# Gate of y in four stages, pooling products kept apart from x and added in the SSD half

## The chip, the cores and the metric

One core of one Trainium2 chip runs the whole program; the time is the device time of that core in microseconds (us). The core has a matmul engine (PE, TensorE), three engines for elementwise work (DVE, ACT, POOL) and a queue, SP, which issues nearly every transfer (DMA) of this kernel, in order. PE writes its results into eight PSUM banks; everything else lies in SBUF tiles. A profile is one execution of the program with its instructions recorded.

## The reference

One layer of a hybrid decoder in float32, for 1056 tokens (1024 of a prompt, 8 x 4 of a decode group). Width 1024, FFN width 2816. What matters here is the mixer and what stands behind it:

```python
x = x + 0.5 * swiglu(rms_norm(x, norm_ffn1), ...)        # FFN1
proj = rms_norm(x, norm_mix) @ w_in                        # z | xBC | dt | pool
y, h = ssd_scan(xs, dtp, a, bm, cm, h0)                     # the scan
y = rms_norm((y + d_skip * xs) * silu(z), ssd_norm_w)       # gate by z, then a norm
yp = multiscale_pool(pool_ext, n_valid, pool_w, pool_scale)
x = x + concat([y, yp], axis=-1) @ w_out                    # w_out has 2048 rows
x = x + 0.5 * swiglu(rms_norm(x, norm_ffn2), ...)           # FFN2
x = x + sigmoid(rms_norm(x, norm_ple) @ ple_gate) * (p @ ple_proj)
y = rms_norm(x, final_norm)
```

The product with `w_out` is taken in two halves: the pooling half (rows of yp) and the SSD half (rows of y). The norm of y is a factor for each token, so the SSD half is multiplied by it after its matmuls.

## The kernel before

Tensors lie with the 1024 channels as eight blocks of 128 partitions (index `m` for output blocks) and tokens along the free side. Tokens are cut into `CH`, pieces of 384, 384 and 288, or into four pieces of `CQ` = 264. float32 accuracy comes from splitting each operand into a high and a low part; `three` (L258) takes three matmul passes for each of eight channel blocks, so one product of one output block with one piece of tokens is 24 matmuls. A weight block is loaded by SP as 512 KB (L216) and split by an ACT cast (L235) and a DVE subtraction (L236).

The stages around the change, in order of time:

- **Scan.** `scan()` runs 16 units. Between them `products()` yields one product at a time (loop at L1259): 24 of z (evicted from their bank by an ACT copy, L1218, and stored to `d_z`) and 24 of the pooling half. A product of the pooling half loads its piece of x from `d_x` (L1232), adds it to the bank on DVE (L1235) and stores the sum to `d_x` (L1236). The scan has 35 yields, so 11 products of the pooling half lie in it and 13 are left. While `products()` runs it has three banks, `nacc[0] = 3`.
- **Mixed stage.** The while loop after the scan takes one product of the pooling half and two steps of `gated()` a turn. `gated()` has 24 steps (three pieces of tokens x eight blocks): it loads z (L1244) and y (L1245), multiplies z by the norm of x on POOL (L1246), takes Silu on ACT (L1247), multiplies y by it on DVE (L1248), splits the result into `yh` (ACT, L274) and `yl` (DVE, L275), squares it on ACT (L1251) and adds the square to `acc` on DVE (L1253). A step takes three buffers of a ring of 13 (`tmp`).
- **SSD half.** L1290 to L1308: eight blocks of four pieces of 264 tokens, 32 products of 24 matmuls on `yh` and `yl`, now with all eight banks, from bank 0 on. Each one loads x (L1298), multiplies the bank by the norm `R1` on DVE (L1301), adds x on POOL (L1302), stores x (L1303), and splits the sum for FFN2 (ACT L274, DVE L275); an ACT square (L282) and a POOL addition (L283) gather the squares for the next norm. The three matmuls of the norm (L289, bank 7) stand among the first four products, each one ahead of the first use of its piece.
- **FFN2's first blocks.** Matmuls L507 write banks 0 to 3 first, then 4 and 5. x is loaded once more (L540) once the ring of buffers is released, and the second norm (L289 to L294) follows.

The order of PE is written out by hand everywhere. The orders of POOL, DVE and ACT are written by hand in the scan and in parts of the FFNs; in the mixed stage and the SSD half a tile scheduler sets them, and that of SP everywhere.

Of the kernel before, what the change touches and what calls it, by code (L numbers as in the profile page):

```python
# [15 lines left out]
P = 128  # L16
D = 1024
KB = 8
# [65 lines left out]
def emit(tc, dr):  # L84
# [25 lines left out]
    def f(o, n, p0=0, p1=P):  # L110
        return o.f[p0:p1, o.c : o.c + n]
# [33 lines left out]
    d_z = dp.tile([P, KB, T], F32, name="d_z")  # L145
    d_yp = dp.tile([P, KB, T], F32, name="d_yp")
    d_yf = dp.tile([P, KB, T], F32, name="d_yf")
    d_ac = dp.tile([P, P], F32, name="d_ac")
    d_acs = dp.tile([H, TS], F32, name="d_acs")

# [5 lines left out]
    def tmp(n):  # L156
        cnt["T"] += 1
        return tslots[cnt["T"] % len(tslots)]
# [1034 lines left out]
    def products():  # L1193
# [32 lines left out]
        for m in range(8):  # L1226
            w = next_w()
            for c0, n in CH:
                while groups and groups[0][1][0] <= c0:
                    take()  # L1230
                t = tslots[4] if m == 0 else tmp(n)
                SY.dma_start(f(t, n), d_x[:, m, c0 : c0 + n])  # L1232
                ps = bank()[:, 0:n]
                gemm_X(ps, w, c0, n)
                V.tensor_tensor(f(t, n), ps, f(t, n), op=ALU.add)  # L1235
                SY.dma_start(d_x[:, m, c0 : c0 + n], f(t, n))  # L1236
                yield

    def gated():

        for c0, n in CH:
            for m in range(8):
                z, yz, q = tmp(n), tmp(n), tmp(n)
                SY.dma_start(f(z, n), d_z[:, m, c0 : c0 + n])  # L1244
                SY.dma_start(f(yz, n), d_yf[:, m, c0 : c0 + n])  # L1245
                G.tensor_tensor(f(z, n), f(z, n), f(o_R0 + c0, n), op=ALU.mult)  # L1246
                S.activation(f(z, n), f(z, n), AF.Silu)  # L1247
                V.tensor_tensor(f(yz, n), f(yz, n), f(z, n), op=ALU.mult)  # L1248
                split_gain(L["yh"] + (m * T + c0), L["yl"] + (m * T + c0), f(yz, n), vec(V_SSD + m), n)
                acc = f(L["acc"] + c0, n)  # L1250
                S.activation(f(q, n) if m else acc, f(yz, n), AF.Square)  # L1251
                if m:
                    V.tensor_tensor(acc, acc, f(q, n), op=ALU.add)  # L1253
                yield

    a, b = scan(), products()
# [17 lines left out]
    while a is not None or b is not None:  # L1274
        if b is not None and next(b, done) is done:
            b = None
        for _ in range(2):
            if a is not None and next(a, done) is done:
                a = None
    later_norm(L["R1"])  # L1280

    def R1_at(c0, n):
        for a, na in CH:
            if a in pending and a < c0 + n:
                finish_norm(*pending.pop(a))
        return f(L["R1"] + c0, n)


    nacc[0] = 8
    cnt["acc"] = 0  # L1290
    for m in range(8):
        w = next_w()
        if m == 7:
            load_raw("wgu2", 0)
        for k in range(4):
            h, c, c0, n = k // 2, k % 2, CQ * k, CQ
            xr, t = tmp(n), tmp(n)
            SY.dma_start(f(xr, n), d_x[:, m, c0 : c0 + n])  # L1298
            ps = bank()[:, 0:n]
            three(ps, [((w(i, 0), w(i, 1)), (r(o_yh + (i * T + c0), n), r(o_yl + (i * T + c0), n))) for i in range(KB)])  # L1300
            V.tensor_tensor(f(t, n), ps, R1_at(c0, n), op=ALU.mult)  # L1301
            G.tensor_tensor(f(t, n), f(t, n), f(xr, n), op=ALU.add)  # L1302
            SY.dma_start(d_x[:, m, c0 : c0 + n], f(t, n))  # L1303
            o = piece(half(m % 2, h), m // 2) + CQ * c
            split_gain(o, o + TH, f(t, n), vec(V_FFN2 + m), n)
            square_into(f(t, n), c0, n, m == 0)
            if m == 7 and k < 2:
                weights1("wgu2", 0, L7["W2"], k)  # L1308
    load_raw("wgu2", 1)


# [185 lines left out]
```

## Time and profile before

| | |
|---|---|
| time, median of 3 runs | 2324.18 us (2323.12 to 2325.68) |
| profiled execution | 2321.62 us, of which the span of the trace is 2319.9 |
| PE busy | 2242.5 us, 97% of the span |
| DVE, ACT, POOL busy | 1436.6, 792.7, 482.8 us (62%, 34%, 21%) |
| chain that ended last | PE 83%, DVE 8%, issue 4%, DMA 3%, ACT 2%, POOL 1% |
| mixed stage | 1294.35 to 1357.33 us |
| SSD half | 1357.33 to 1455.41 us, then FFN2 |

PE is the engine that sets the time, with gaps in a few places. The profiled execution lies 2.56 us below the median of the runs shown; 1.7 us of it lie around the span. A busy PE is not always at full speed: the granted clock (PEclk, 1.00 is full) is read beside it. Times of instructions on POOL are rough. Where the text says what an engine waited for, it is the releaser that the trace infers from semaphores.

### The profile page before, as it was taken

What the parts mean: (1) busy time and instruction counts of PE and PEld (TensorE: products, weight loads), DVE (VectorE), ACT (ScalarE), POOL (GpSimd) and SP (SyncE); (2) the same over time, 40 slices, a digit from 0 to 9 for tenths busy, and PEclk for the clock granted to TensorE, in tenths of its full rate; (3) what the DMA queues carried; (4) which work ended last, traced back from release to release, by engine and by line L of the source; (5) the groups of instructions that cost most, each with busy time, mean ns of one, the idle gap of its engine ahead of it and who ended that gap; (6) DMA issues with size and microseconds to landing.
All of it is one profiled execution on the core that took longest, in us unless ns stands there. A gap on an engine that the chain in (4) does not pass through costs nothing.

```text
span 2319.9 us, 38096 instructions
## 1 busy us (share of the span) xinstructions
PE 2242.5 (97%) x15651; PEld 2188.1 (94%) x15651; DVE 1436.6 (62%) x2113; ACT 792.7 (34%) x1331; POOL 482.8 (21%) x416
## 2 busy tenths in 40 slices
PE   8999999999999999999979989999999999999997
PEld 8999999999999999977858889999999999999996
DVE  7776666663345856545777764576766666334566
ACT  6422222231123124223453543342222233112455
POOL 1122222200003420022222335112222220001343
PEclk9999999999999999999989999999999999999999
DMA  5422122282122233344354654432221227221243
GB/s 185 140 79 79 67 82 84 78 268 84 60 83 85 70 90 68 49 136 144 117 155 135 201 171 140 178 123 79 83 79 69 80 91 255 83 76 44 72 148 130
DMA packets 155711, 257.48 MB, mean 111 GB/s; under 512 B 56784, under 2 KB 101008, under 8 KB 150032
## 3 DMA queue, kind: packets, MB, share of 16 engines
q1 hardware_dynamic: 155536, 255.04, 34.5%
q8 instruction: 123, 2.02, 0.3%
q14 instruction: 52, 0.43, 0.1%
HBM read 195.42 MB, written 59.57 MB: 110 GB/s over the span
## 4 chain that ended last, share of the span: by engine, by line
PE 83%; DVE 8%; issue 4%; DMA 3%; ACT 2%; POOL 1%; SPq 0%; DVEq 0%; ACTq 0%; POOLq 0%
PE bank L258 42%; PE pair L390 32%; PE bank L507 5%; PE bank L1162 1%; DVE Wa L1004 1%; DMA Wa<-d_ac 1%; DVE wl L1150 1%; ACT xs L1014 1%; PE bank L1064 1%; DVE Wa L1105 1%; DMA tmp<-d_z 1%; DMA raw<-wgu 0%; DVE W L379 0%; PE bank L875 0%; PE bank L289 0%
## 5 line engine op out<-in xcount | busy, mean ns | idle before, releaser
L258 PE MATMUL bank<-X,W 128*128 128x384 f32 (+1 forms) x4320 | 730.3, 325 | 17.2 <-DVE W L236 5.3
L258 PEld LDWEIGHTS bank<-X,W 128*128 128x128 f32 x4320 | 702.5, 189 | 21.6 <-DVE W L236 6.0
L390 PE MATMUL pair<-X,W 128*128 128x264 f32 x3648 | 458.4, 285 | 0.2 <-DVE n L415 0.2
L390 PEld LDWEIGHTS pair<-X,W 128*128 128x128 f32 x3648 | 450.8, 188 | 0.5 <-DVE n L415 0.4
L390 PE MATMUL pair<-E,W 128*128 128x264 f32 x1824 | 234.9, 285 | 0.0
L390 PEld LDWEIGHTS pair<-E,W 128*128 128x128 f32 x1824 | 227.5, 188 | 0.0
L488 DVE SCALAR_TENSOR_TENSOR x<-bank,x 128x384 f32<-128x384 f32 (+1 forms) x192 | 99.4, 523 | 205.9 <-PE bank L258 203.7
L258 PE MATMUL bank<-E,W 128*128 128x384 f32 (+1 forms) x1200 | 217.3, 323 | 0.0
L258 PEld LDWEIGHTS bank<-E,W 128*128 128x128 f32 x1200 | 197.0, 188 | 0.0
L283 POOL TENSOR_TENSOR acc<-acc,tmp 128x384 f32<-128x384 f32 (+2 forms) x89 | 82.6, 928 | 498.2 <-ACT tmp L282 498.2
L379 DVE TENSOR_TENSOR W<-ws,W 128x512 fp32r<-128x512 f32 x152 | 129.8, 855 | 46.0 <-ACT W L378 45.8
L507 PE MATMUL bank<-X,W 128*128 128x264 f32 x1152 | 146.4, 289 | 6.8 <-DVE acc L292 2.1
L507 PEld LDWEIGHTS bank<-X,W 128*128 128x128 f32 x1152 | 144.2, 192 | 9.2 <-DVE acc L292 2.7
L459 ACT CAST W<-raw 128x640 fp32r<-128x640 f32 (+1 forms) x64 | 50.0, 782 | 249.4 <-PE bank L258 211.2
L420 POOL TENSOR_TENSOR cg<-cg 128x528 f32<-128x528 f32 x38 | 76.0, 2001 | 255.4 <-issue 227.2
L378 ACT CAST W<-ws 128x512 fp32r<-128x512 f32 x152 | 93.1, 615 | 92.0 <-PE pair L390 84.2
L390 PE MATMUL pair<-nd,W 128*128 128x264 f32 x912 | 119.5, 288 | 3.6 <-DVE p L409 3.6
L390 PEld LDWEIGHTS pair<-nd,W 128*128 128x128 f32 x912 | 115.7, 191 | 4.0 <-DVE p L409 4.0
L378 ACT CAST W<-raw 128x512 fp32r<-128x512 f32 x114 | 70.9, 622 | 141.4 <-DMA raw<-wgu 107.1
L258 PE MATMUL bank<-nd,W 128*128 128x384 f32 (+1 forms) x576 | 108.3, 323 | 0.0
L258 PE MATMUL bank<-yh,W 128*128 128x264 f32 x512 | 96.8, 291 | 5.9 <-DVE tmp L1235 5.9
L235 ACT CAST W<-raw 128x1024 fp32r<-128x1024 f32 (+2 forms) x65 | 60.5, 930 | 123.2 <-PE bank L258 109.6
(305 smaller groups left out, 3000.8 us busy)
## 6 DMA issues: line engine op xcount, KB each, us to landing
raw<-wgu SPq DMA_DIRECT2D x43, 1024.0 KB, 4.8
hraw<-d_h SPq DMA_DIRECT2D x44, 528.0 KB, 3.9
d_h<-cg SPq DMA_DIRECT2D x76, 264.0 KB, 2.0
raw<-win SPq DMA_DIRECT2D x28, 512.0 KB, 5.3
raw<-wd SPq DMA_DIRECT2D x32, 384.0 KB, 3.1
raw<-wd SPq DMA_DIRECT2D x32, 320.0 KB, 3.0
Wa<-d_ac SPq DMA_DIRECT2D x16, 512.0 KB, 3.9
raw<-wout SPq DMA_DIRECT2D x16, 512.0 KB, 3.8
```

The lines of the kernel that those rows point to most:

```text
L235: S.copy(r(o_w, n), f(o_r, n))
L258: PE.matmul(ps, lhsT=a, rhs=b, start=i == 0, stop=i == n - 1)
L283: eng.tensor_tensor(f(L["acc"] + c0, n), f(L["acc"] + c0, n), f(o_q, n), op=ALU.add)
L378: S.copy(r(o, 512), f(src, 512))
L379: V.tensor_tensor(r(o + 512, 512), f(src, 512), f(o, 512), op=ALU.subtract)
L390: PE.matmul(ps, lhsT=r(w + (512 * p + P * q), P), rhs=r(x + TH * b, CQ), start=first and q == 0 and j == 0, stop=q == 3 and j == 2, skip_g ...
L420: G.tensor_tensor(f(o_u1, TH), f(o_u1, TH), f(o_g, TH), op=ALU.mult)
L459: S.copy(r(o, n), src)
L488: V.scalar_tensor_tensor(xm, ps, 0.5, xm, op0=ALU.mult, op1=ALU.add)
L507: PE.matmul(ps, lhsT=r(w, P), rhs=r(piece(half(j, h), q) + (TH * b + CQ * c), CQ), start=q + j + i == 0, stop=q == 3 and j == 1 and i == 2)
L1004: V.tensor_scalar(ab3[:, h, :], ab3[:, h, :], f(o_ac + hh + h, 1, 0, nt), 0.0, op0=ALU.subtract, op1=ALU.min)
L1014: S.copy(xs3[q0:q1, 2 * i : 2 * i + 2, :], src)
```

## The change

- **Pooling half.** The product is evicted by an ACT copy (L1235) and stored without x in a new tensor `d_pp` (L1236). The load of x and the DVE addition go: of two transfers one is left.
- **Gate.** `gated()` becomes a pipeline of four parts with delays of 0, 2, 3 and 4 steps: loads, gate (POOL, Silu), upper (DVE product, `yh`, square) and lower (`yl`, `acc`). The square is written over z, so a step takes two buffers of the ring and not three.
- **SSD half.** A product loads x and `d_pp` (L1307, L1308), and POOL adds them ahead (L1311). After the matmuls DVE multiplies the bank by the norm (L1316), POOL adds (L1317), and the rest is as before. SP has three transfers for each product where it had two. The buffers of the sum are o_x and o_p.
- **Start of the SSD half.** The first product takes bank 3 and not bank 0; the matmuls of the norm stand behind the first four products, on banks 7, 0 and 1.

```diff
+    d_pp = dp.tile([P, KB, T], F32, name="d_pp")
     (products, pooling half)
-                SY.dma_start(f(t, n), d_x[:, m, c0 : c0 + n])
                 ps = bank()[:, 0:n]
                 gemm_X(ps, w, c0, n)
-                V.tensor_tensor(f(t, n), ps, f(t, n), op=ALU.add)
-                SY.dma_start(d_x[:, m, c0 : c0 + n], f(t, n))
+                S.copy(f(t, n), ps)
+                SY.dma_start(d_pp[:, m, c0 : c0 + n], f(t, n))
     (gated)
+        def load(k):
+            c0, n, m = steps[k]
+            z, yz = bufs[k] = tmp(n), tmp(n)
+            SY.dma_start(f(z, n), d_z[:, m, c0 : c0 + n])
+            SY.dma_start(f(yz, n), d_yf[:, m, c0 : c0 + n])
+        def gate(k):
+            (c0, n, m), (z, yz) = steps[k], bufs[k]
+            G.tensor_tensor(f(z, n), f(z, n), f(o_R0 + c0, n), op=ALU.mult)
+            S.activation(f(z, n), f(z, n), AF.Silu)
+        def upper(k):
+            (c0, n, m), (z, yz) = steps[k], bufs[k]
+            V.tensor_tensor(f(yz, n), f(yz, n), f(z, n), op=ALU.mult)
+            S.activation(r(L["yh"] + (m * T + c0), n), f(yz, n), AF.Copy, scale=vec(V_SSD + m))
+            S.activation(f(z, n) if m else f(L["acc"] + c0, n), f(yz, n), AF.Square)
+        def lower(k):
+            (c0, n, m), (z, yz) = steps[k], bufs[k]
+            o = m * T + c0
+            V.scalar_tensor_tensor(r(L["yl"] + o, n), f(yz, n), vec(V_SSD + m), f(L["yh"] + o, n), op0=ALU.mult, op1=ALU.subtract)
+            if m:
+                acc = f(L["acc"] + c0, n)
+                V.tensor_tensor(acc, acc, f(z, n), op=ALU.add)
+        for k in range(len(steps) + 4):
+            for part, late in ((load, 0), (gate, 2), (upper, 3), (lower, 4)):
+                if 0 <= k - late < len(steps):
+                    part(k - late)
+            if k > 2:
+                yield
     (SSD half)
-    cnt["acc"] = 0
+    cnt["acc"] = 3
+    def ssd_product(m, w, c0, n):
+        o_x, o_p = tmp(n), tmp(n)
+        SY.dma_start(f(o_x, n), d_x[:, m, c0 : c0 + n])
+        SY.dma_start(f(o_p, n), d_pp[:, m, c0 : c0 + n])
+        ps = bank()[:, 0:n]
+        three(ps, [((w(i, 0), w(i, 1)), (r(o_yh + (i * T + c0), n), r(o_yl + (i * T + c0), n))) for i in range(KB)])
+        G.tensor_tensor(f(o_x, n), f(o_x, n), f(o_p, n), op=ALU.add)
+        return ps, o_x, o_p
+    def ssd_out(m, k, ps, o_x, o_p):
+        h, c, c0, n = k // 2, k % 2, CQ * k, CQ
+        V.tensor_tensor(f(o_p, n), ps, f(L["R1"] + c0, n), op=ALU.mult)
+        G.tensor_tensor(f(o_x, n), f(o_x, n), f(o_p, n), op=ALU.add)
+        SY.dma_start(d_x[:, m, c0 : c0 + n], f(o_x, n))
         ...
+        if m == 0:
+            made = [ssd_product(m, w, CQ * k, CQ) for k in range(4)]
+            for b_, (c0, n) in zip((7, 0, 1), CH):
+                finish_norm(L["R1"], c0, n, b_)
+            for k in range(4):
+                ssd_out(m, k, *made[k])
+        else:
+            for k in range(4):
+                ssd_out(m, k, *ssd_product(m, w, CQ * k, CQ))
```

Three places of the orders follow. In the names the last number of a bank tells the bank: 4818 is bank 0 before, 4819 is bank 0 after, and they count up from there. A row with x24 is 24 matmuls.

PE where the last three products of the pooling half end and the SSD half begins, before:

```order
L258 MATMUL bank_23_4819<-X_70,W_69 128x384 x24
L258 MATMUL bank_23_4820<-X_70,W_69 128x384 x24
L258 MATMUL bank_23_4818<-X_70,W_69 128x288 x24
L258 MATMUL bank_23_4818<-yh_11114,W_69 128x264 x2
L258 MATMUL bank_23_4818<-yl_11115,W_69 128x264
```

and after:

```order
L259 MATMUL bank_23_4820<-X_70,W_69 128x384 x24
L259 MATMUL bank_23_4821<-X_70,W_69 128x384 x24
L259 MATMUL bank_23_4819<-X_70,W_69 128x288 x24
L259 MATMUL bank_23_4822<-yh_11104,W_69 128x264 x2
L259 MATMUL bank_23_4822<-yl_11105,W_69 128x264
```

The first SSD product wrote the bank of the pooling product just ahead of it; it now writes bank 3, which no product of the stage used.

PE where the last SSD product ends and FFN2 begins, before:

```order
L258 MATMUL bank_23_4825<-yh_11114,W_69 128x264 x2
L258 MATMUL bank_23_4825<-yl_11115,W_69 128x264
L507 MATMUL bank_23_4818<-X_70,W_63_11110 128x264
L507 MATMUL bank_23_4819<-X_70,W_63_11110 128x264
L507 MATMUL bank_23_4820<-X_70,W_63_11110 128x264
L507 MATMUL bank_23_4821<-X_70,W_63_11110 128x264
```

and after:

```order
L259 MATMUL bank_23_4821<-yh_11104,W_69 128x264 x2
L259 MATMUL bank_23_4821<-yl_11105,W_69 128x264
L508 MATMUL bank_23_4819<-X_70,W_63_11100 128x264
L508 MATMUL bank_23_4820<-X_70,W_63_11100 128x264
L508 MATMUL bank_23_4821<-X_70,W_63_11100 128x264
L508 MATMUL bank_23_4822<-X_70,W_63_11100 128x264
```

The last SSD product was in bank 7 and is now in bank 2, so FFN2's first matmuls write the banks of the last three products (0, 1, 2), where they wrote the banks of products four and more places back.

POOL in the middle of the SSD half (output blocks 3 and 4), before: the addition of x (L1302) and of the squares (L283) alternate.

```order
L283 TENSOR_TENSOR acc_11106<-acc_11106,tmp_66_11116 128x264
L1302 TENSOR_TENSOR tmp_66_11116<-tmp_66_11116 128x264
L283 TENSOR_TENSOR acc_11106<-acc_11106,tmp_66 128x264
L1302 TENSOR_TENSOR tmp_66<-tmp_66 128x264
L283 TENSOR_TENSOR acc_11106<-acc_11106,tmp_66 128x264
```

and after:

```order
L284 TENSOR_TENSOR acc_11096<-acc_11096,tmp_66 128x264
L1317 TENSOR_TENSOR tmp_66<-tmp_66,tmp_66_11106 128x264
L1311 TENSOR_TENSOR tmp_66_11106<-tmp_66_11106 128x264
L284 TENSOR_TENSOR acc_11096<-acc_11096,tmp_66_11106 128x264
L1311 TENSOR_TENSOR tmp_66<-tmp_66 128x264
L1317 TENSOR_TENSOR tmp_66_11106<-tmp_66_11106 128x264
L284 TENSOR_TENSOR acc_11096<-acc_11096,tmp_66_11106 128x264
L1311 TENSOR_TENSOR tmp_66<-tmp_66 128x264
L1317 TENSOR_TENSOR tmp_66_11106<-tmp_66_11106 128x264
```

The new addition L1311 of a later product stands in two positions: behind L1317, ahead of the squares L284, or behind L284, ahead of the next L1317. From the seventh product on there are 26 of them: 8 in the first position, 18 in the second. The first six stand ahead of the first L1317, and the first six L1317 follow in a row.

## Rows read from the trace of the kernel before

**Rows 1.** Windows: us, each engine's busy time (instructions), PEclk, DMA share, GB/s.

```profile
1294.35:1357.33 62.98, 52.28 (x315) 51.25 (x314) 51.81 (x84) 37.31 (x77) 26.58 (x23) 0.97 0.78 240
1357.33:1455.41 98.08, 98.08 (x774) 97.32 (x775) 45.93 (x81) 36.93 (x75) 43.63 (x57) 0.97 0.42 131
```

**Rows 2.** Timeline of PE: start, duration, work, count, idle time before and its releaser.

```profile
1294.47 38.49 PE L258 MATMUL bank<-X,W 128*128 128x288 f32 x240
...
1333.86 4.45 PE L258 MATMUL bank<-X,W 128*128 128x384 f32 x24 [0.91 <-ACT tmp L1251]
1342.18 9.23 PE L258 MATMUL bank<-X,W 128*128 128x384 f32 x48 [3.87 <-DVE tmp L1235]
1357.33 0.78 PE L258 MATMUL bank<-yh,W 128*128 128x264 f32 x2 [5.93 <-DVE tmp L1235]
...
1362.75 1.07 PE L289 MATMUL bank<-acc,cst 128*128 128x384 f32 x2
```

**Rows 3.** Waits of SP, 1294 to 1357: us in total, times, longest.

```profile
SPq L1236 <- DVE tmp L1235: 15.4, 10, 2.4
```

**Rows 4.** Groups by line, 1294 to 1357: busy us, mean ns; idle before.

```profile
L274 ACT ACTIVATE yh<-tmp,vec 128x384 fp32r<-128x384 f32 (+1 forms) x23 | 13.5, 587 | 12.4 <-DVE tmp L1248 10.0 <-DMA d_yf<-xs 2.4
L1247 ACT ACTIVATE tmp<-tmp 128x384 f32<-128x384 f32 (+1 forms) x23 | 11.2, 493 | 13.0 <-POOL tmp L1246 12.9
L1251 ACT ACTIVATE tmp<-tmp 128x384 f32<-128x384 f32 (+1 forms) x20 | 9.7, 487 | 0.0
L235 ACT CAST W<-raw 128x1024 fp32r<-128x1024 f32 x5 | 5.2, 1034 | 0.0
L1235 DVE TENSOR_TENSOR tmp<-bank,tmp 128x384 f32<-128x384 f32 (+1 forms) x13 | 6.6, 508 | 0.0
```

**Rows 5.** ACT's copies of z from the bank, group by line, 1080 to 1194.

```profile
L1218 ACT COPY tmp<-bank 128x384 f32<-128x384 f32 (+1 forms) x14 | 6.3, 451 | 6.8 <-PE bank L258 5.8 <-ACT xdh L1113 0.8
```

**Rows 6.** Transfers, 1294 to 1357: size, median us from issue to landing.

```profile
tmp<-d_x SPq DMA_DIRECT2D x8, 192.0 KB, 3.4
d_x<-tmp SPq DMA_DIRECT2D x8, 192.0 KB, 2.8
```

**Rows 7.** Windows of two pairs of scan units, with z and with pooling products.

```profile
1148.68:1173.58 24.90, 22.00 (x135) 19.32 (x134) 19.47 (x35) 11.55 (x23) 6.90 (x6) 1.00 0.37 123
1239.10:1265.33 26.23, 23.35 (x136) 20.92 (x135) 20.70 (x38) 12.30 (x24) 7.67 (x6) 0.93 0.41 125
```

**Rows 8.** Timeline of DVE: the norm ahead of the SSD half's first output.

```profile
1364.48 0.56 DVE L292 SCALAR_TENSOR_TENSOR acc<-bank,R 128x384 f32<-128x384 f32 x1 [5.29 <-ACT R L290]
1366.26 0.43 DVE L1301 TENSOR_TENSOR tmp<-bank,R 128x264 f32<-128x264 f32 x1
```

**Rows 9.** Timeline of POOL in the SSD half.

```profile
1443.40 1.67 POOL L1302 TENSOR_TENSOR tmp<-tmp 128x264 f32<-128x264 f32 x1 [2.27 <-DVE tmp L1301]
...
1455.97 0.77 POOL L283 TENSOR_TENSOR acc<-acc,tmp 128x264 f32<-128x264 f32 x1 [1.01 <-ACT tmp L282]
1456.69 0.76 POOL L1302 TENSOR_TENSOR tmp<-tmp,tmp 128x264 f32<-128x264 f32 x1
1458.45 0.75 POOL L283 TENSOR_TENSOR acc<-acc,tmp 128x264 f32<-128x264 f32 x1 [1.00 <-ACT tmp L282]
```

**Rows 10.** Transfers, 1370 to 1455.

```profile
d_x<-tmp SPq DMA_DIRECT2D x30, 132.0 KB, 1.8
tmp<-d_x SPq DMA_DIRECT2D x26, 132.0 KB, 2.1
raw<-wout SPq DMA_DIRECT2D x4, 512.0 KB, 3.4
```

**Rows 11.** DVE groups by line, 1370 to 1458: the lowerings of weights.

```profile
L236 DVE TENSOR_TENSOR W<-raw,W 128x1024 fp32r<-128x1024 f32 x6 | 8.0, 1328 | 3.9 <-ACT W L235 3.9
L514 DVE TENSOR_TENSOR W<-raw,W 128x1024 fp32r<-128x1024 f32 x3 | 4.2, 1390 | 1.7 <-ACT W L513 1.7
```

**Rows 12.** Timeline of PE: FFN2's first matmuls.

```profile
1455.41 17.69 PE L507 MATMUL bank<-X,W 128*128 128x264 f32 x144
```

More of the change, by code (lines that the diff above doesn't have):

```diff
@@ L1231, in products @@
                 t = tslots[4] if m == 0 else tmp(n)
-                SY.dma_start(f(t, n), d_x[:, m, c0 : c0 + n])
                 ps = bank()[:, 0:n]
                 gemm_X(ps, w, c0, n)
-                V.tensor_tensor(f(t, n), ps, f(t, n), op=ALU.add)
-                SY.dma_start(d_x[:, m, c0 : c0 + n], f(t, n))
+                S.copy(f(t, n), ps)
+                SY.dma_start(d_pp[:, m, c0 : c0 + n], f(t, n))
                 yield
     def gated():
[L1241 to L1249, printed above, removed]
-                acc = f(L["acc"] + c0, n)
-                S.activation(f(q, n) if m else acc, f(yz, n), AF.Square)
-                if m:
-                    V.tensor_tensor(acc, acc, f(q, n), op=ALU.add)
@@ new lines, in gated @@
+        steps = [(c0, n, m) for c0, n in CH for m in range(8)]
+        bufs = {}
+        def load(k):
[7 more added lines that the diff above has]
+            S.activation(f(z, n), f(z, n), AF.Silu)
@@ L1279, in emit @@
                 a = None
[L1280 to L1286, printed above, removed]
-    nacc[0] = 8
-    cnt["acc"] = 0
+    nacc[0] = 8
+    cnt["acc"] = 3
[12 more added lines that the diff above has]
+        SY.dma_start(d_x[:, m, c0 : c0 + n], f(o_x, n))
+        o = piece(half(m % 2, h), m // 2) + CQ * c
+        split_gain(o, o + TH, f(o_x, n), vec(V_FFN2 + m), n)
+        square_into(f(o_x, n), c0, n, m == 0)
+        if m == 7 and k < 2:
+            weights1("wgu2", 0, L7["W2"], k)
     for m in range(8):
@@ L1294, in emit @@
             load_raw("wgu2", 0)
[L1295 to L1308, printed above, removed]
+        if m == 0:
[7 more added lines that the diff above has]
+                ssd_out(m, k, *ssd_product(m, w, CQ * k, CQ))
     load_raw("wgu2", 1)
```

## The prediction

> **What bounds the kernel now.** I read the windows of the two stages first, then PE's gaps in its timeline and waits, then the engines that end those gaps, and last the place where the moved work goes: POOL and the transfers of the SSD half.
>
> The mixed stage takes 62.98 us, the SSD half 98.08 us [rows 1]. In the first PE runs ten products without a gap in 38.49 us and then stops three times: 0.91 us for a buffer that ACT had to read, 3.87 and 5.93 us for a bank that DVE had to empty in L1235 [rows 2]. Behind the stops PE is slower: the first SSD product with its 24 matmuls runs from 1357.33 to the norm's matmul at 1362.75, 5.4 us [rows 2], where FFN2's matmuls of the same size go at 24 in 2.95 us [rows 12]. The granted clock is 0.97 in the mean of each stage [rows 1], so it is lost in few places, and these are the places. How long would the 13 products take with no stop? The first ten are six of 384 and four of 288 tokens, 3456 columns of tokens in 38.49 us, 11.14 ns a column; the last three have 1056, 11.8 us; together 50.3. So the stage holds 62.9 - 50.3 = 12.6 us that can be won.
>
> Why is the bank emptied late? DVE is busy 51.8 of 63 us [rows 1] and L1235 stands in its order among the gate's instructions; SP, with all loads of the gate behind it, waits ten times for L1235 to finish before it may store, 15.4 us in all [rows 3]. So the pooling half and the gate hold each other up through DVE and SP. In the SSD half PE is never idle (98.08 busy of 98.08 [rows 1]): a change there gains nothing on PE but the slow first product, and can only lose.
>
> A difference of 0.2% (4.6 us) is about what a measurement of this kernel can tell from no change.
>
> **Mixed stage.** Off DVE go 13 additions, 6.6 us [rows 4]; off SP and the transfers go 13 loads of x, which took 3.4 us each to land and which L1235 needed before it could start [rows 6]. To ACT come 13 copies at 0.451 us [rows 5], 5.9 us. ACT's list is then 13.5 + 11.2 + 9.7 + 1.5 (the three squares into acc) for the gate, 5.2 for casts [rows 4], and 5.9: 47.0 us. DVE's is 51.8 - 6.6 = 45.2. Both fit under 50.3, but ACT only just: it idled 25 us in the stage on DVE's and POOL's results [rows 4], and the four parts with delays must take most of that away. Ends: 50.3 (ACT never late) and 58 (47.0 plus half of those 25 us less the overlap that the earlier loads give, about 11). I take 52.5, nearer to the first, because SP's 15.4 us of waits ends with a copy that waits for PE alone, and because the first SSD products no longer wait for a bank: bank 3 has been free all along. Gain 10.5, between 5 and 12.6.
>
> **Scan.** Eleven products of the pooling half lie in it. A pair of units with them took 26.23 us where a pair with z products, which ACT copies out, took 24.90 [rows 7]: 1.3 us a pair. Between two and three pairs hold pooling products, so -3; the first gate moves ahead of the last unit's exponential on ACT and takes two loads of an activation table there, in idle time of ACT. I take -2.5, from 0 to -5.
>
> **SSD half: the gain at its start.** The first product at full clock takes 24 x 122 ns = 2.93 us (about the pace of FFN2's 144 matmuls, 17.69 us [rows 12]), so 32 products are 94 us and three norms 1.5: PE could be through at S + 95.6, S being the stage's start, where it was 98.1.
>
> **SSD half: POOL.** This is where the work went. 32 additions at 0.75 us [rows 9] are 24 us more. Whether they cost depends on their place. Between the start of L1302 and that of L283 lie 1.76 us, of which 1.00 is idle, waiting for ACT's square; from L283 to the next addition 0.72 [rows 9]. So one step can repeat after 2.48 us, and PE's 2.93 covers it. An addition L1311 in the idle 1.00 is free; one between L283 and the next L1317 makes the step 2.48 + 0.72 = 3.20, longer than PE's. In the new order of POOL 18 of the last 26 stand there.
>
> Start: four products (11.7 us), then the norm. From the norm's matmul to the first L1301 it took 1366.26 - 1362.75 = 3.5 us [rows 2, 8]; now seven instructions of the norm and not three stand ahead on DVE, 4 x 0.56 more [rows 8]. So the first product is multiplied at S + 17.4 and the first L1317 starts at S + 18. Six follow in a row (4.3), and the load for the seventh is queued on SP behind the store of the sixth: 2.1 to land [rows 10], some 0.5 of issue and 1.5 for two additions L1311. The seventh L1317 is at S + 27. Then 25 steps of 2.48 and 16 delays of 0.72 (two of the 18 lie before): 73.5, so the last at S + 100.5, and the last bank is emptied just before it, at S + 100. Eight banks keep PE going until its products are done (95.6). But FFN2's first matmuls now write the banks of the last three products, so PE waits for that last multiplication: 100 where FFN2 began at 98.1. **Base: +2**.
>
> Three surcharges follow. First, **transfers**: the second load of product j + 4 takes the buffer that the store of product j leaves, and its L1311 stands before the L1317 of j + 2. Two steps of 3.20 less 0.75 leave 5.65 us for 0.75 + store + load + some 0.3 of issue, so store and load may take 4.6 together. In the SSD half they took 1.8 + 2.1 = 3.9; in the mixed stage, at a DMA share of 0.78, 2.8 + 3.4 = 6.2 [rows 1, 6, 10]. The share here was 0.42 with two transfers a product and will be near 0.57 with three. In the middle, 5.05, each pair of steps is 0.45 late, 13 pairs, 6 us; the ends are 0 and 13 x 1.6 = 21. I take 5. Second, **DVE and POOL together**: beside a weight lowering an addition on POOL took 1.67 us and not 0.76 [rows 9]. There are nine lowerings [rows 11], one of which hit POOL; POOL goes from 44% to near 70% busy. Two hits: +2, from 1 to 8. Third, **the clock** behind PE's idle time: after 5.93 us of idling the first product lost 5.4 - 2.93 = 2.5 us [rows 2]; FFN2 will start behind 4 to 12 us of it. +2.5, from 0 to 3.
>
> On the second surcharge a page has a sharper rule. The row shows one of nine collisions. The Trainium skill, "SBUF — State Buffer", section "SBUF: two separate sides", says that DVE with two SBUF inputs and GpSimd share a port pair under an exclusive lock for the whole instruction and that the loser fully blocks. By it every lowering that meets POOL's work costs POOL its whole length. The 1.67 us row agrees; how often it happens no row of this case shows, and the third rival prices it at every time.
>
> **The sum**, against the profiled 2321.62: mixed stage -10.5, scan -2.5, SSD half +2 + 5 + 2 + 2.5 = +11.5. That is -1.5, 2320.1; the median lies 2.56 above the profiled execution: **2322.7**. No other line changes; the second norm's chain after FFN2's first 17.69 us [rows 12] shifts with x's last store, which is no later than PE is.
>
> **The rivals.**
> 1. *POOL's additions find room.* If the transfers are early and two in three additions slip into the idle 1.00 us (each also needs its loads by then), the SSD half stays bound by PE or close to it: +2 in place of +11.5, with the mixed stage as above: 2324.2 - 13 + 2 = 2313. For it: POOL's work is only 44 + 24 of 98 us. Against: engines run in order, and the order puts 18 of 26 in the wrong place.
> 2. *The buffer loop decides, slower.* Store and load of 6.2 us together, as in the mixed stage, make every pair of steps 1.6 us late: +21 in place of +5, 2322.7 + 16 = 2339. It decides from 4.6 us; half-way it gives 2331. For it: weight loads of 512 KB (3.4 us [rows 10]) share the queue, and six or seven fall in the stage. Against: medians of 1.8 and 2.1.
> 3. *Every lowering stops POOL*: nine times 0.91 us, +8.2 in place of +2, 2329.
> 4. *The change does not free PE*: ACT's copies come as late as DVE's additions, because they stand behind Silu and squares that wait. The mixed stage keeps 5 of its 10.5: 2328.
>
> **How the numbers follow.** Forecast (2318 to 2328) 0.48; rival 1 0.23; rival 2 0.11; rival 3 0.08; rival 4 0.10. Faster by over 0.2% is under 2319.5: all of rival 1 and a fifth of the forecast, 0.33. Slower is over 2328.8: rival 2, half of 3 and 4, a little of the forecast, 0.25. The rest, 0.42, is within 0.2%. The predicted time is 2322.7. The range of 8 in 10 takes in rival 1 with a scan gain of 4, 2311, and the half-way form of rival 2 with some of the others, 2333.
>
> **What would show it.** In the profile after, PE should stand in the mixed stage for less than 3 us in all and begin the SSD half about 13 us earlier than 1357.3. The releaser of FFN2's first matmul should be DVE's L1316, with 4 to 14 us of idle before it, and POOL's L1317 should come every 3.2 us or more with L1311 right ahead of it. If L1317 is spaced 2.9 us, rival 1 is right; if POOL's L1311 wait for transfers of d_pp for more than 10 us, rival 2. If PE still waits for L1235 in the mixed stage, now on ACT, it is rival 4. I am wrong altogether if the SSD half shows PE waiting inside it, between its products, since I count eight banks as enough.

## The result: 0.54% slower, and the profile after

The changed kernel takes 2336.3 us in the median of five runs (2334.11 to 2341.25) against 2323.3 for the kernel before (2321.69 to 2325.68, five runs): a ratio of 1.0054, 95% interval [1.0044, 1.0065]. The profiled execution took 2338.49 us, 16.9 above the profiled one of before.

The windows of the two stages answer to [rows 1]; the second one runs to the third start of FFN2's matmuls:

```profile
1296.22:1350.96 54.74, 50.73 (x314) 49.53 (x313) 49.78 (x70) 39.25 (x85) 26.02 (x23) 1.00 0.73 219
1350.96:1465.56 114.60, 99.14 (x778) 96.75 (x776) 46.27 (x84) 38.91 (x80) 73.22 (x90) 0.95 0.52 158
```

The mixed stage fell to 54.7 us; counted in the same way, from its first matmul in [rows 2], it took 62.9 before. The SSD half rose from 98.08 to 114.60, with POOL busy 73 us of it where it had been 44. PE's timeline, which answers to [rows 2, 12], shows what ended PE's waits:

```profile
1296.22 30.81 PE L259 MATMUL bank<-X,W 128*128 128x288 f32 x192
1327.66 4.48 PE L259 MATMUL bank<-X,W 128*128 128x384 f32 x24 [0.63 <-ACT tmp L1235]
1332.85 3.44 PE L259 MATMUL bank<-X,W 128*128 128x288 f32 x24 [0.71 <-ACT tmp L1235]
1337.37 4.47 PE L259 MATMUL bank<-X,W 128*128 128x384 f32 x24 [1.08 <-ACT tmp L1235]
1343.44 7.68 PE L259 MATMUL bank<-X,W 128*128 128x384 f32 x48 [1.60 <-ACT tmp L1235]
1350.96 0.41 PE L259 MATMUL bank<-yh,W 128*128 128x264 f32 x2
...
1460.19 0.56 PE L508 MATMUL bank<-X,W 128*128 128x264 f32 x1 [6.13 <-DVE tmp L1316]
1463.17 0.59 PE L508 MATMUL bank<-X,W 128*128 128x264 f32 x1 [2.42 <-DVE tmp L1316]
1465.56 20.11 PE L508 MATMUL bank<-X,W 128*128 128x264 f32 x142 [1.80 <-DVE tmp L1316]
1485.51 1.29 PE L290 MATMUL bank<-acc,cst 128*128 128x384 f32 x4
...
1490.59 4.63 PE L508 MATMUL bank<-X,W 128*128 128x264 f32 x24 [2.09 <-DVE acc L293]
```

The last row is FFN2's second start, behind the second norm. Before, it came 12.6 us earlier:

```profile
1478.02 2.19 PE L507 MATMUL bank<-X,W 128*128 128x264 f32 x13 [2.09 <-DVE acc L292]
```

In the mixed stage four short stops for ACT's copy (4.0 us) stand where three stops of 10.7 us stood, and there is no stop at the SSD half's start. At the end of the SSD half PE stands three times for L1316, once for each of the banks 0, 1 and 2, and the 142 matmuls behind it take 20.11 us where 144 took 17.69; the granted clock is 0.50, the lower of PE's two levels, from 1460 to 1470, behind the stops, and 1.00 from 1472 on.

Between its products PE also stands four times inside the SSD half, 5.1 us in all (waits of PE in that stage):

```profile
PE bank L259 <- DVE W L237: 2.4, 2, 1.3
PE bank L259 <- DVE acc L293: 1.8, 1, 1.8
PE bank L259 <- ACT W L236: 0.9, 1, 0.9
```

The second line is the fifth product, which takes bank 7 just behind the norm's matmul; the others are weight blocks that were split late. These stops do not set the end of the stage: PE's last product is through at 1454.1, and its bank is emptied by L1316 only at 1465.5.

POOL's timeline, which answers to [rows 9], in the middle and at the end of the SSD half:

```profile
1396.59 1.75 POOL L1317 TENSOR_TENSOR tmp<-tmp 128x264 f32<-128x264 f32 x1
1399.29 0.76 POOL L284 TENSOR_TENSOR acc<-acc,tmp 128x264 f32<-128x264 f32 x1 [0.94 <-ACT tmp L283]
1400.13 0.75 POOL L1311 TENSOR_TENSOR tmp<-tmp 128x264 f32<-128x264 f32 x1
1400.84 0.76 POOL L1317 TENSOR_TENSOR tmp<-tmp 128x264 f32<-128x264 f32 x1
1402.54 0.76 POOL L284 TENSOR_TENSOR acc<-acc,tmp 128x264 f32<-128x264 f32 x1 [0.94 <-ACT tmp L283]
1403.25 0.75 POOL L1317 TENSOR_TENSOR tmp<-tmp,tmp 128x264 f32<-128x264 f32 x1
1405.25 0.75 POOL L1311 TENSOR_TENSOR tmp<-tmp 128x264 f32<-128x264 f32 x1 [1.24 <-DMA tmp<-d_pp]
...
1465.73 0.75 POOL L1317 TENSOR_TENSOR tmp<-tmp 128x264 f32<-128x264 f32 x1
```

Three things are to be seen: L1311 between L284 and L1317, the idle 0.94 us ahead of L284 left empty; an addition of 1.75 us beside a weight lowering; and a wait for d_pp. POOL's waits from the seventh L1317 to the last (us in total, times, longest):

```profile
POOL acc L284 <- ACT tmp L283: 17.1, 19, 0.9
POOL tmp L1311 <- DMA tmp<-d_pp: 6.4, 8, 1.2
POOL tmp L1317 <- DVE tmp L1316: 1.6, 1, 1.6
```

Where the 16.9 us of the two profiles lie, by PE's matmuls and each rounded: +2.5 before the scan, -0.8 in it, -8.1 in the mixed stage, +18.9 from the SSD half's start to FFN2's second start, +4.3 behind that. The first and the last of these lie in code that the change leaves alone. Over the profiles below the first varies from -2.6 to +2.6 and the last from -2.5 to +0.5, so single profiles differ by a few microseconds without a cause in the change, and the timed +13 is the better figure for the whole.

### The profile page after: what moved, and what is told of

The parts are those of the page before. It is cut to its first block, busy times and chain, and to the rows that moved or that the text cites. A ratio compares the mean times of both kernels' runs of the same rounds, so it can differ in the third digit from the quotient of the medians.

```text
span 2336.7 us, 38114 instructions
## 1 busy us (share of the span) xinstructions
PE 2251.1 (96%) x15651; PEld 2194.4 (94%) x15651; DVE 1427.9 (61%) x2089; ACT 802.6 (34%) x1357; POOL 510.8 (22%) x448
## 4 chain that ended last, share of the span: by engine, by line
PE 77%; DVE 7%; DMA 6%; issue 4%; POOL 3%; ACT 3%; SPq 0%; DVEq 0%; POOLq 0%; ACTq 0%
PE bank L259 38%; PE pair L391 31%; PE bank L508 5%; PE bank L1163 1%; POOL tmp L1317 1%; DMA Wa<-d_ac 1%; DMA hraw<-d_h 1%; DMA raw<-wgu 1%; DVE wl L1151 1%; DVE Wa L1005 1%; POOL tmp L1311 1%; DMA tmp<-d_pp 1%; DVE Wa L1106 1%; POOL acc L284 0%; ACT xs L1015 0%
## 5 line engine op out<-in xcount | busy, mean ns | idle before, releaser
L284 POOL TENSOR_TENSOR acc<-acc,tmp 128x384 f32<-128x384 f32 (+2 forms) x89 | 82.8, 930 | 493.7 <-ACT tmp L283 493.5
```

Source lines behind the costliest of these rows:

```text
L284: eng.tensor_tensor(f(L["acc"] + c0, n), f(L["acc"] + c0, n), f(o_q, n), op=ALU.add)
```

## Experiments

Ratios are to the kernel before, timed on the same chip. "Stage cost" is the time from the first SSD matmul to FFN2's second start, against 120.7 us in the profile of before; for the changed kernel it is +18.9. It comes from one profile of each run.

### What of the SSD half costs: the load or the addition

**no_preadd**: neither.

```diff
-        SY.dma_start(f(o_p, n), d_pp[:, m, c0 : c0 + n])
-        G.tensor_tensor(f(o_x, n), f(o_x, n), f(o_p, n), op=ALU.add)
```

> The changed kernel without the load of d_pp (L1308) and without the addition L1311; the pooling half's part of the output is left out. Everything else is as changed. Theory P (POOL's order, its lock with DVE, and the buffer loop make the SSD half late): the last L1316 comes with PE's last product, the SSD half costs 96 to 99 us instead of 114.6, and of the +13 us against the kernel before some 22 go: 2312 to 2316. Rival B (the banks at FFN2's start are the cause, whatever POOL does): PE still stands for 8 us or more ahead of L508, 2328 or more. Rival M (the mixed stage did not gain in a timed run): 2323.

Measured: 0.9974 [0.9964, 0.9984], stage cost +1.8. **load_only** drops only the second of these lines.

> The changed kernel with the load of d_pp kept and L1311 left out, so the pooling half's part of the output is left out: the transfers are those of the changed kernel, POOL's work that of the kernel before. Theory P1: within 3 us of the run without load and addition. Rival T (the loop of store and load through the same buffers): the multiplication L1316 waits for the load in place of L1311, and 6 us or more stay, 2320 or more.

Measured: 0.9971 [0.9961, 0.9981], stage cost +1.0. **add_only** drops the first and lets L1311 add x to itself.

> The changed kernel without the load of d_pp, with L1311 kept on POOL: it adds x to itself, so the pooling half's part is left out and x counts twice. POOL's work is that of the changed kernel, the transfers are those of the kernel before. Theory P1 (POOL's place and lock are most of the loss, 0.72 us for 16 to 18 additions and 0.9 for six to nine lowerings): 2328 to 2333. Rival T (late transfers of d_pp are most of it): within 3 us of the run without L1311.

Measured: 1.0075 [1.0058, 1.0092], stage cost +22.8. So the third transfer of each product costs nothing as long as no addition waits for it, and the addition brings the loss, here more than in the whole change. This run has an order of its own, though: without the load the scheduler put nearly every L1311 ahead of the squares, where it waits for x. POOL's timeline of add_only (L1310 is the addition, L1316 the old one):

```profile
1411.54 0.63 POOL L1310 TENSOR_TENSOR tmp<-tmp 128x264 f32<-128x264 f32 x1 [1.42 <-DMA tmp<-d_x]
1412.12 0.75 POOL L284 TENSOR_TENSOR acc<-acc,tmp 128x264 f32<-128x264 f32 x1
1412.83 0.75 POOL L1316 TENSOR_TENSOR tmp<-tmp 128x264 f32<-128x264 f32 x1
1415.03 0.63 POOL L1310 TENSOR_TENSOR tmp<-tmp 128x264 f32<-128x264 f32 x1 [1.45 <-DMA tmp<-d_x]
```

The period is 3.5 us: a load waits for a buffer that the squares free, the addition waits for the load, and the squares wait behind the addition. A wait for a transfer that cost nothing while only L1302 needed x became a link of POOL's loop.

### Is it POOL's amount of work, the lock with DVE, the buffers or the order?

**squares_dve** moves the squares off POOL.

```diff
-        square_into(f(o_x, n), c0, n, m == 0)
+        square_into(f(o_x, n), c0, n, m == 0, V)
```

> The changed kernel, whole, with the addition of the squares (L284) in the SSD half on DVE instead of POOL: 28 instructions of about 0.45 to 0.5 us move to an engine that was busy 42 of 103 us. Theory P: POOL has 64 additions of 0.75 = 48 us left and no wait for ACT's square between them, so the step falls from 3.43 to PE's 2.93: 2313 to 2320. Rival T: the loop of store and load stays and the lock with DVE is met more often: 2326 or more.

Measured: 1.0037 [1.0024, 1.0050], stage cost +16.6, although POOL lost nearly a third of its instructions. The expected fall to PE's pace did not come. POOL's timeline shows the next chain:

```profile
1401.20 0.75 POOL L1317 TENSOR_TENSOR tmp<-tmp 128x264 f32<-128x264 f32 x1
1403.86 0.75 POOL L1317 TENSOR_TENSOR tmp<-tmp,tmp 128x264 f32<-128x264 f32 x1 [1.91 <-DVE tmp L1316]
1404.97 0.75 POOL L1311 TENSOR_TENSOR tmp<-tmp 128x264 f32<-128x264 f32 x1 [0.37 <-DMA tmp<-d_pp]
...
1409.36 0.90 POOL L1311 TENSOR_TENSOR tmp<-tmp 128x264 f32<-128x264 f32 x1 [1.14 <-DMA tmp<-d_pp]
```

L1316 of the next product stands on DVE behind the split L276 of this one, which waits for ACT, which waits for POOL. From the L1317 at 1401.20 to the next this circle takes 2.66 us before L1311 adds anything, and loads still come late.

**no_lower** leaves DVE's weight lowering out in the SSD half.

```diff
+            if not L.get("ssd"):
                 V.tensor_tensor(r(o_w + n, n), f(o_r, n), f(o_w, n), op=ALU.subtract)
```

> The changed kernel without the lowering of the weights (L237 on DVE) for the blocks that are made in the SSD half; the low parts of these weights are left as they were, so the matmuls multiply wrong numbers, with everything else and the whole timing as it is. Theory K (each lowering on DVE stops an addition on POOL, some 1.0 us for six to seven of them, and POOL is the bound): 6 to 8 us faster than the changed kernel, some 6 us above the kernel before. Rival: the additions only shift, and the time changes by less than 3 us.

Measured: 1.0038 [1.0026, 1.0050], that is 8.7 us above the kernel before, where the changed kernel lay 13.0 above its own runs of before: some 4.3 us back where 6 to 8 were expected, and a stage cost of +12.1. L1317's group (here L1319) has a mean of 0.78 us where it had 0.93, so the lowerings are what stretched it. The changed kernel, then this run:

```profile
L1317 POOL TENSOR_TENSOR tmp<-tmp 128x264 f32<-128x264 f32 x26 | 24.2, 935 | 3.6 <-DVE tmp L1316 3.6
L1319 POOL TENSOR_TENSOR tmp<-tmp 128x264 f32<-128x264 f32 x27 | 21.0, 781 | 8.4 <-DVE tmp L1318 8.4
```

**sq_in_op** writes the square into o_p (two buffers a product); **after18** cuts the ring into 18 buffers of 264 tokens over the same room.

```diff
+    tslots[:] = [o_T2 + CQ * i for i in range(11)] + [wide[0] + CQ * i for i in range(7)]
```

> The changed kernel, whole, with the square written into the second buffer of the sum, so that a product takes two buffers of the ring and not three; the scheduler's order of POOL stays nearly as it was, additions L1311 between L284 and L1317. Theory T (the loop store, load through the same buffer): the waits of L1311 for transfers of d_pp go (they were 14.8 us in all) and 6 to 9 of the 13 us come back. Theory O: the order still makes the step 3.2 us and lowerings still stop POOL; 2 to 6 us come back.

> The changed kernel, whole, with only the ring of the SSD half cut into 18 buffers of 264 tokens; the orders are the scheduler's. Theory T2: the waits for d_pp (14.8 us) go. If they are what holds POOL there too, 8 us or more of the 13 come back; if the place of L1311 in POOL's order does (theory O), 2 to 6, since 16 additions of 0.72 us still lie between L284 and L1317 and lowerings still stop POOL.

Measured: 1.0045 [1.0027, 1.0063] and 1.0028 [1.0017, 1.0038], stage costs +17.1 and +15.4. More buffers give back 2 and 6 us, as much as was expected if the order is what holds POOL, and less than if the transfers were; POOL still waits 17.6 and 20.4 us for ACT's squares, in the order that did not change.

**ordered** writes the order of POOL, DVE and ACT by hand:

```diff
+    with tc.manual_schedule(engines=MS):
+        for s in range(32 + 5):
...
+            if 0 <= s - 4 < 32:
+                ssd_out(*made[s - 4])
+            if 0 <= s - 5 < 32:
+                ssd_tail(*made[s - 5])
```

Ahead of these lines step s issues product s with its L1311 (and after the fourth the norms); `ssd_out` is L1316, L1317 and the store, `ssd_tail` the split and the squares, with the square in o_p.

> The changed kernel, whole, with the same instructions, but the orders of POOL, DVE and ACT in the SSD half written out by hand: for each product L1311 of that product, then L1316 and L1317 of the product four back, then the split and the squares of the product five back; the square goes into the second buffer of the sum, so a product takes two buffers of 13 and not three. Theory O (what costs is the place of L1311, between waits of a chain through four engines, not POOL's 72 us of work nor its lock with DVE): the step falls below PE's 2.93 us and the SSD half costs 96 to 100 us instead of 114.6: 9 to 13 us faster than the kernel before, about 2308 to 2312 where that runs at 2320. Rival L (POOL's work and its lock with DVE cost by themselves): 2322 or more.

Measured: 1.0097 [1.0076, 1.0118], the slowest of all, where a gain of 9 to 13 us was expected. The waits for ACT's squares went (0.3 us left), and the ring took their place (POOL's and PE's waits):

```profile
POOL tmp L1311 <- DMA tmp<-d_pp: 32.8, 14, 4.6
```

```profile
PE bank L508 <- ACT W L514: 21.6, 1, 21.6
```

A product now holds its buffers over six steps, 12 of 13. With 18 narrow ones:

> The run with the orders written by hand, and the ring of the SSD half cut into 18 buffers of 264 tokens, the width that is used there, in the place of 13 of 384. In the run with 13, POOL waited 32.8 us for loads of d_pp, every second product, in one loop of store, load and addition. Theory T2 (with the order mended, the ring is what holds POOL): these waits go below 6 us, the SSD half takes 96 to 100 us, and the time is 8 to 13 us below the kernel before. Rival L (POOL's work, its lock with DVE): POOL stays late with its own additions, and the time stays above the kernel before.

Measured: 0.9995 [0.9985, 1.0004]; the waits for d_pp are 7.1 us and the last SSD matmul comes 9.2 us earlier than before. Against after18, timed on the same chip with as many buffers and the scheduler's order, this is 8.7 us faster (2322.76 against 2331.49): so much the order is worth once buffers suffice, with the square in o_p, which is part of it. The 8 to 13 us below the kernel before did not come. PE waits again, for the second split of FFN2's weights (first line) and for a bank (last line); the second line is the mixed stage, the third the second norm:

```profile
PE bank L508 <- ACT W L514: 4.6, 1, 4.6
PE bank L259 <- ACT tmp L1235: 4.1, 4, 1.7
PE bank L508 <- DVE acc L293: 2.1, 1, 2.1
PE bank L508 <- DVE tmp L1318: 1.8, 1, 1.8
```

**ordered18w** puts that split earlier (`if s in (29, 30): weights1(...)`).

> The run with hand-written orders and 18 buffers, with the two splits of FFN2's first weights put four products earlier in the order. There the SSD half ended 9.2 us earlier than in the kernel before, but PE then waited 6.4 us for the second split and for the last bank. Theory O (with the additions of POOL in their place and buffers enough, the second addition costs nothing): FFN2 starts 6 to 9 us earlier than in the kernel before and the time is 5 to 9 us below it, 0.2 to 0.4%. Rival L: POOL's 96 additions and its lock with DVE keep the last product late wherever the splits stand, and the time stays within 3 us of the kernel before.

Measured: 0.9994 [0.9985, 1.0003]. The wait for the split went, that for the banks grew to 4.3 us. FFN2 starts 8.4 us earlier than before, as expected, but two more stops and slower matmuls behind that start (19.41 us for 142, where 17.4 is the old pace) take 5 us of it again. The time falls by 2.2 us and not by 5 to 9, which is the rival's number, though not for its reason: the last product was not late.

### The banks

**bank0** begins on bank 0 again, with the norms on 5, 6 and 7; **after_b** does the same and moves the mixed stage's products to banks 5 to 7, so that bank 0 is free at the start.

```diff
-    cnt["acc"] = 3
+    cnt["acc"] = 0
-            for b_, (c0, n) in zip((7, 0, 1), CH):
+            for b_, (c0, n) in zip((5, 6, 7), CH):
```

> The changed kernel, whole, with the SSD half beginning on bank 0 as before, and the norms on banks 5, 6 and 7; FFN2's first matmuls find banks 0 to 3 free. Theory P (POOL is late, the bank only passes it on): PE starts FFN2 some 10 us earlier, but x's last store and the reload of x behind it are as late as before, so the norm's end moves by only 2 to 5 us, and at the SSD half's start some wait for bank 0 comes back: 0 to 4 us faster than the changed kernel. Rival B (the banks are the cause): 10 us or more faster than the changed kernel.

> The changed kernel with only the banks turned round in the same way, so that no wait for bank 0 at the SSD half's start comes back (as it did in the run that began on bank 0). Theory P: FFN2 starts some 9 us earlier but x's last store stays late, and 3 to 6 of the 13 us come back. Rival B (the banks were the cause): 10 us or more come back.

Measured: 1.0048 [1.0033, 1.0063] and 1.0032 [1.0021, 1.0043]. In after_b FFN2 starts at 1452.01 where the changed kernel had 1460.19, but the wait moves on: PE's timeline

```profile
1454.87 4.46 PE L510 MATMUL bank<-X,W 128*128 128x264 f32 x22 [2.33 <-DVE tmp L1319]
1460.36 14.73 PE L510 MATMUL bank<-X,W 128*128 128x264 f32 x119 [1.03 <-DVE tmp L1319]
1474.93 1.29 PE L292 MATMUL bank<-acc,cst 128*128 128x384 f32 x4
1483.33 1.65 PE L292 MATMUL bank<-acc,cst 128*128 128x384 f32 x2 [7.11 <-DVE acc L295]
```

has 7.11 us at the second norm, whose DVE work stands behind the splits of the reloaded x, which waits for the last store. Some 4.5 of 13 us come back (8.5 above the kernel before), so the banks mostly pass POOL's lateness on; of themselves they are about a third of the loss. In bank0 only 1 us comes back; there PE waits 1.72 us for bank 0 at the SSD half's start.

With the order mended, ordered18w still waits for the banks: **ordered18b** joins ordered18w and after_b's banks, **ordered18c** also has the outputs three products back instead of four.

> The last run with hand-written orders, with the banks turned round: the 13 products of the mixed stage take banks 5, 6 and 7, the SSD half begins on bank 0 (still free) and ends on bank 7, the norms take banks 5, 6 and 7. So FFN2's first matmuls find banks 0 to 3 free, as in the kernel before. Theory B2 (in that run the last thing left was FFN2's wait for the last three products' banks, 4.3 us, and the slower matmuls behind it, 1.9): 4 to 6 us faster than that run, 0.25 to 0.35% below the kernel before. Rival: x's last store and reload bound the second norm instead, and less than 2 us come back.

> The same with the outputs three products behind the additions L1311 and not four. Theory: outputs end a product earlier, so x's reload and the second norm do; 0 to 2 us faster than with four. Rival: with three the loads of d_pp have less time, POOL waits for them more, and it is slower by 1 to 4 us.

Measured: 0.9983 [0.9974, 0.9992] and **0.9960 [0.9948, 0.9973]**. In ordered18b the waits for banks went, but PE stands 4.6 us at the second norm, and of the 4 to 6 us expected against ordered18w some 1.3 come, as the rival had it. The last run is faster than both kernels: 2310.91 us in the median where the kernel before took 2318.95. Its window from the first SSD matmul to the last and PE's timeline behind it:

```profile
1350.30:1445.50 95.20, 95.20 (x775) 94.56 (x774) 42.00 (x80) 36.27 (x74) 67.26 (x83) 1.00 0.61 184
```

```profile
1445.63 17.69 PE L510 MATMUL bank<-X,W 128*128 128x264 f32 x144
1463.15 1.29 PE L292 MATMUL bank<-acc,cst 128*128 128x384 f32 x4
1466.91 0.91 PE L292 MATMUL bank<-acc,cst 128*128 128x384 f32 x2 [2.47 <-DVE acc L295]
```

PE is never idle, at full clock, with POOL busy 67 of 95 us. Three products back are 4.5 us faster than four, where 0 to 2 were expected. In the profiles 2.2 of it lie in the stage cost (+1.1 with four, -1.1 with three), with the wait at the second norm 2.5 us instead of 4.6, which is what was expected; the rest lies in code that is the same in both, where profiles differ by as much. The waits of L1311 for d_pp are 2.5 us, with four they are 7.2.

### The mixed stage

**gate_only** has the new gate and nothing else; **old_gate** has everything but the new gate.

> The kernel before with only gated() replaced by the four stages with two buffers a step; the pooling half keeps its load of x, its addition on DVE and its store, and the SSD half is that of the kernel before. Theory G (the gate's buffers and order were what held DVE and SP): PE's stop in the mixed stage falls from 10.7 to 2 to 5 us and the time by 4 to 8 us. Rival E (DVE's eviction behind the gate was what held PE, so the copy on ACT was needed): within 3 us of the kernel before.

> The changed kernel with the old gated(), three buffers a step and no stages. The SSD half is the changed one. Theory E (the copy on ACT frees PE in the mixed stage, with the old gate too): the SSD half begins as early as in the changed kernel within 3 us, and the time is that of the changed kernel. Theory G2 (both are needed, since a copy behind a gate that waits is as late as an addition on DVE): PE stops in the mixed stage for 8 us or more, the SSD half begins 6 to 9 us later, and so does the end.

Measured: 0.9998 [0.9988, 1.0008] and 1.0043 [1.0026, 1.0060]. PE's waits of gate_only in and behind the mixed stage:

```profile
PE bank L258 <- DVE tmp L1235: 11.0, 3, 4.9
```

That is as much as before (10.7 with the one for ACT). From the end of the scan to the SSD half's start, the gate alone changes +1.2 us, the copy on ACT alone -6.0, both -8.1: the eviction on DVE behind the gate was what held PE. Whether the new gate adds anything to the copy isn't shown. In the eleven other profiles whose mixed stage is that of the changed kernel it takes 54.8 to 59.5 us, a gain of 8.1 to 3.4 with 7.8 in the middle, and the timed loss of old_gate (10.8 us) is no larger than that of the changed kernel.

**pool_adds_x** and **pool_adds_x2** keep x in the mixed stage: ACT copies, POOL adds (13 products).

```diff
-                V.tensor_tensor(f(t, n), ps, f(t, n), op=ALU.add)
+                t2 = tmp(n)
+                S.copy(f(t2, n), ps)
+                G.tensor_tensor(f(t, n), f(t, n), f(t2, n), op=ALU.add)
```

> Another way to the gain of the mixed stage: x is loaded there as before, the product is copied out of its bank by ACT into a buffer of its own, and POOL, 27 of 63 us busy there, adds x; 13 products so, the 11 in the scan as before; four-stage gate; no d_pp, and the SSD half of the kernel before, from bank 3 on. By theory P (the loss lies in the second addition of the SSD half alone) the SSD half then costs what it did, the mixed stage gains 6 to 9 us as in the changed kernel, and the time is 5 to 9 us below the kernel before. Rival: POOL, in order, becomes the bound of the mixed stage (13 times 1.28 us more, next to DVE): no gain, within 3 us of the kernel before.

> x added by POOL in the mixed stage, now with delays of 0, 1, 2 and 3 steps in the gate, so that no buffer of the ring of 13 comes round while its step still needs it (in the run before this it did). 13 products are copied by ACT and added to x by POOL, the SSD half is that of the kernel before but for its first bank. Theory P: the SSD half costs what it did and the mixed stage gains 5 to 9 us: 0.2 to 0.4% faster than the kernel before. Rival: POOL waits for loads of x and for ACT's copies, with the gate's products behind it, and the gate ends so late that the norm holds PE up: no gain or a loss.

Measured: 1.0014 [1.0003, 1.0025] and 1.0018 [1.0010, 1.0027]. In the first a gate step's buffer was taken for another product before the step had used it, so part of the gated y is overwritten and its waits are partly false ones. The second has none of that; its SSD half began 4.5 us earlier than before, and 5.5 us went in waits of PE for the first norm, behind a gate that ended late. So the rival held: POOL becomes part of the gate's chain, and nothing is gained.

## Why the prediction was wrong

The forecast was 2322.7 us, and 2336.3 were measured. The step that failed is the surcharges on the SSD half: the prediction put transfers, lowerings and clock at 5 + 2 + 2.5 = 9.5 us, and the trace has 8.4 + 5.8 + 2.7 = 16.9. The first two, which lie on POOL's chain, were too small; the third was right. With the base of +2 that makes the +18.9 of the stage, where the forecast had +11.5. Point by point, with the terms as they were put:

- *Surcharge of DVE and POOL, "two hits: +2"*: after the seventh L1317 eight weight lowerings met POOL's work. Six of them held an L1317, at 1.61 to 1.75 us, 5.8 us in all, where one of nine had before [rows 9, 11]. At the other two the addition on POOL had begun first, and the lowering was the one that took longer. So the third rival, which prices every lowering, was nearer: POOL is now busy most of the time, and every lowering met it. no_lower, which leaves the lowerings out, gives 4.3 us back.
- *Surcharge of the transfers, +5*: 6.4 us from the seventh L1317 on, and with the two late microseconds at the start 8.4.
- *Surcharge of the clock, +2.5*: 20.11 - 17.44 (142 matmuls at the old pace) = 2.7, as forecast.
- *Base: the last bank emptied at S + 100*: the first L1317 came at S + 18.5 (18 forecast), the seventh at S + 29.0 (27, though the terms given for it add up to 26.4). From there to the last it took 85.8 us in place of 73.5. The difference of 12.3 is the 6.4 and the 5.8 above, so the pace of POOL's order itself, 2.48 and 3.20 us a step, was right.
- *Mixed stage -10.5, between 5 and 12.6*: -8.1. Right in mechanism (old_gate shows the copy does it) and a little large: ACT's copies still cost four stops of 4.0 us. *Scan -2.5*: -0.8 in this profile, and from -2.3 to +3.5 in eleven others with the same scan, so that gain is not shown. The two gave 8.9 in place of 13.
- *First product at full clock, no wait for a bank*: shown by the timeline; the 24 matmuls from 1350.96 run at 0.12 us each.

The two on POOL were weighed one by one, from a kernel in which POOL had idle time between its instructions, and taken at their middle and low end. They are not independent: once POOL is the chain that ends last, what had been absorbed in idle time is added in full. The SSD half and FFN2's start give +18.9, the mixed stage and the scan -8.9; that is 3 us less than the timed +13, about what single profiles differ by.

- *Rival 2* (the buffer loop, slower) named the right side, and its 2331 to 2339 holds the result. By the letter its sign came true too: L1311 waits 14.8 us for d_pp in the whole half, more than 10. But 8.4 of these lie before the seventh L1317, 6.5 of them in one wait that ended while the first L1317 still stood behind the norm. Late transfers are some 8 of the 19 us, so that its number holds the result is in part luck. load_only shows that the transfers by themselves cost nothing, and add_only that they cost when POOL's order makes additions wait for them.
- *The signs*: PE's stops in the mixed stage are 4.0 us (less than 3 was said), and the SSD half begins 6.4 us earlier (about 13 was said). FFN2's first matmul waits for L1316 for 6.1 us, and L1317 comes every 3.4 us, both as said. "Wrong altogether if PE waits inside the SSD half" was also met, with 5.1 us, but not for the reason given there: no product waited for L1316 to empty a bank. One waited for a bank that a norm had used, three for weights.
- *"PE is never idle in the SSD half, so a change there can only lose"* and *"the base is POOL's place in the order"* held: with nearly the same instructions in another order, 18 buffers and the banks turned, the stage takes 95.2 us for PE, the 95.6 of the forecast.

What the runs do not separate is how the loss divides between order, buffers, banks and lowerings. Taking lowerings away gives back 4.3 us, buffers 6, the banks 4.5; they overlap. The order by hand costs 12 us with 13 buffers (ordered against sq_in_op) and gives 9 with 18 (ordered18 against after18).

## What to carry to other kernels

An operation that is taken off a loaded stage is not free in a stage where PE is busy all the time. Count there the chain of waits on the engine that receives it, in order, and not its busy share: with POOL at 67 of 95 us it was free in one order, with buffers enough and the banks turned, and in another the stage cost 19 us more. When an engine becomes the one that ends last, price everything that it used to absorb (locks with a neighbour, late loads, a bank passed on) at its full length and together. And an order in steps needs buffers not only for the steps that it holds, but also for the store and the load between two uses of a buffer: the order that held 12 of 13 buffers was the slowest run, with 18 it was as fast as the kernel before, and with the banks turned faster.

## What was not expected of the hardware

A weight lowering on DVE takes 1.22 to 1.23 us where no addition on POOL has begun ahead of it (ordered18). In the changed kernel it stretched an addition on POOL from 0.75 us to between 1.61 and 1.75 at six of eight meetings; at the other two the addition had begun first, kept its 0.75 us, and the lowering took 1.65 and 1.71. The Trainium skill, "SBUF — State Buffer", section "SBUF: two separate sides", says that whichever of the two starts first gets the shared port pair for its whole instruction and that the other fully blocks. The trace agrees at these eight meetings: the price falls on DVE as well as on POOL. The smaller split on DVE (0.49 us) comes with additions of POOL that are 1.01 to 1.03 us long in the hand-ordered runs, for most products; in ordered18c, where PE never stands in the stage, that cost nothing.
